# Keeping the last two expert blocks' rows on chip and adding them with one-hot products in the final norm

## The chip, the cores and the metric

The kernel runs on one core of a Trainium2 chip. A core has a matrix engine (TensorE, PE in the profile), a vector engine (VectorE, DVE), an activation engine (ScalarE, ACT), GpSimd (POOL), and SyncE (SP), whose queue starts most transfers. The metric is the device time of one launch in microseconds, as a median of several runs.

## The reference

One transformer block of 1024 latent tokens and 256 context tokens, 1024 wide: a mixer (gated delta rule and a gated recurrence), then a mixture of 32 experts of which each token uses two, and after each of the two a residual sum with a layer norm. Only the last part is touched by the change:

```python
def post_norm(r, g, b):
    return (layer_norm(r) * g + b).astype(r.dtype)
...
    x = post_norm(DEEP_ALPHA * x + gt1_l * u_l, ln_g[l, 0], ln_b[l, 0])
    f_l = hierarchical_moe(modulate(x, sh2_l, sc2_l).reshape(B * L, D), *moe_args).reshape(B, L, D)
    x = post_norm(DEEP_ALPHA * x + gt2_l * f_l, ln_g[l, 1], ln_b[l, 1])
```

The expert sum `f_l` of a token has two terms, one for each expert that it uses, each scaled by its router weight.

## The kernel before

The mixer and the routing take the first 870 us or so and stay as they are. Then come 22 blocks of up to 128 token slots, in the order of the table `ORDER`. A block holds the tokens of one to four experts ("pieces"). For each block the loop of `make`, `up`, `turn` and `down` gathers token rows from DRAM (`gather`, POOL), transposes them (`pf`, `xT`), multiplies by the up weights (`pu`), applies the gate (`hid`), transposes (`hT`) and multiplies by the down weights (`py`). VectorE scales the product by router weight and gate into a tile `y`, in two halves of 512 columns (line 1536).

`acc` is a DRAM tensor of 1024 rows that starts as the scaled residual. `down` adds the rows of `y` to it with one indirect transfer from POOL's queue for each piece (line 1539), each of which reads, adds and writes the rows that the table names (`rows_to`, or `tbri` for a block of one piece). They follow each other: each waits until the one before has landed. The next to last block has two pieces, the last has one.

Behind the blocks stands a loop over overflow blocks (line 1601), whose count of rounds is read on the chip; with these inputs no round is run, but all engines meet there and wait for all transfers and all engines. Behind it, SP loads `acc` as eight tiles of 128 tokens (line 1640, tiles named `u` as they lie in the places of the expert weights), and the final layer norm runs on each tile: sums and squares (`bn_stats` on VectorE, lines 1657 and 1658, or two passes on ScalarE, lines 1650 and 1651), a first pass `(x - mean) * g` (line 1660), the inverse root (`rsqrt_pool`, lines 149 to 157 on GpSimd, for two tiles at once; the last pair on VectorE, lines 129 to 139), and a second pass `x * rs + b` (line 1671 on VectorE, or lines 1668 and 1669 on ScalarE and GpSimd for three tiles). SP stores each half tile (line 1674). The norm's gain and bias rows are loaded ahead of the overflow loop (lines 1632 and 1633).

A scheduler sets the order on each engine from a timing model, so the order of the rows below is the program's, not the code's.

Of the kernel before, what the change touches and what calls it, by code (L numbers as in the profile page):

```python
# [9 lines left out]
F32 = mybir.dt.float32  # L10
# [8 lines left out]
P = 128  # L19
D = 1024  # L20
# [59 lines left out]
YB = 3  # L80
DEPTH = 2
PA = {'ORD': 'x0 z1 x1 g0 z2 z0 x2 x3 g1 g2 g3 z3', 'ZB': 'qvsa', 'ADV1': 1, 'ADV2': 2, 'PER': 1, 'A0': 0, 'SQB': 1, 'GELU': 0, 'GSTG': 1, 'PM': (4, 4), 'HIV': (3, 8, 10, 14, 17, 20, 23), 'LOV': (2, 4, 21), 'C1V': (0, 1, 3, 4, 5, 14, 15, 19, 23), 'PSS': 0, 'TOK': (('kt', 4), ('v', 4)), 'EMV': 0, 'RGV': 0, 'CVB': 3, 'WRB': 3, 'HO': 'kvq', 'SQP': 0, 'YMA': 0}

UNITS = 18

# [2 lines left out]
def hybrid_block(ctx, tc, x, c, ctx_in, c_ctx, w_ada, b_ada, w_in, conv_qkv_w, dn_a_log, dn_dt_bias, dn_onorm_w,  # L88
# [1346 lines left out]
    scs.close()  # L1435
    pss.close()

    psm = ctx.enter_context(tc.tile_pool(name="psm", bufs=1, space=PSUM, reuse_waits="tile"))
    me = ctx.enter_context(tc.tile_pool(name="me", bufs=1, side="right", reuse_waits="tile"))
    more[0] = psm  # L1440
    ptab = psm.tile([P, 512], F32, name="ptab", tag="ptab")
# [16 lines left out]
    route_last()  # L1458
    ri, wslot = rows_of(ptab, NBLK, "tb")
    sb_moe["routed"] = wo  # L1460
    rows_to = T_([P, 4, NBLK - ONE], "rows_to", I32)
    V.tensor_tensor(rows_to, ptab[:, None, ONE:NBLK].to_broadcast([P, 4, NBLK - ONE]), onl, op=ALU.add)

# [8 lines left out]
    class Block:  # L1472
# [50 lines left out]
            self.hT = sb.tile([P, 2, P], F32, name="hT", tag="hT", bufs=2)  # L1523
            nc.scalar.copy(self.hT[:, :, 0:u], pt[:, 0:256].rearrange("p (f t) -> p f t", t=P)[:, :, 0:u])  # L1524

        def down(self, ws):
            u = self.used
            turn = self.in_turn()
            y = sb.tile([P, D], F32, name="y", tag="y", bufs=YB)
            for q in range(2):  # L1530
                qs = slice(q * 512, (q + 1) * 512)
                py = psm.tile([P, 512], F32, name="py", tag="py", bufs=3)
                for f in range(2):
                    for r, o, n in parts(self.pieces):
                        turn(nc.tensor.matmul(py[o:o + n, :], self.hT[:, f, o:o + n], ws[r][:, f, qs], start=f == 0, stop=f == 1))  # L1535
                nc.vector.scalar_tensor_tensor(y[0:u, qs], py[0:u, :], self.weights[0:u], gt2[0:u, qs], op0=ALU.mult, op1=ALU.mult)  # L1536

            for (r, o, n), to in zip(self.pieces, self.to):
                nc.gpsimd.indirect_dma_start(out=acc, out_offset=bass.IndirectOffsetOnAxis(ap=to[0:o + n], axis=0), in_=y[0:o + n], in_offset=None,  # L1539
                                             bounds_check=NL - 1, oob_is_err=False, compute_op=ALU.add)  # L1540

    blocks = []

    def make(i):
        if i < NBLK:
# [9 lines left out]
    for i in range(NBLK + 1):  # L1555
        if i < NBLK:
            blocks[i].up(W)
            ahead(i, i - 2)
        if i > 0:
            blocks[i - 1].down(Wd)  # L1560
            ahead(min(i, NBLK - 1), i - 1)
        if i + 1 < NBLK:
            blocks[i + 1].transpose()
            make(i + 3)
        if i < NBLK:
            blocks[i].turn()
# [68 lines left out]
    for i in range(4):  # L1635
        x2 = place(4 + i, [P, 2, D])
        for q in range(2):
            t = 2 * i + q
            xs.append(x2[:, q, :])
            nc.sync.dma_start(xs[t], acc[t * P:(t + 1) * P, :])  # L1640
    mv = cst.tile([P, 8, 2], F32, name="mv3")
    rs = cst.tile([P, 8], F32, name="rs3")
    for t0 in range(0, 8, 2):
        ts, two = (t0, t0 + 1), slice(t0, t0 + 2)
        for t in ts:
            x_, mean, var = xs[t], mv[:, t, 0:1], mv[:, t, 1:2]
            if t in (3, 5, 6, 7):
                sq = sb.tile([P, D], F32, name="sq2", tag="y", bufs=YB)
                nm = small([P, 1], "nm3")
                nc.scalar.activation(sq, x_, AF.Identity, scale=-1.0 / D, accum_out=nm)  # L1650
                nc.scalar.activation(sq, x_, AF.Square, bias=nm, accum_out=var)
                nc.vector.tensor_scalar_mul(var, var, 1.0 / D)
                nc.vector.tensor_scalar_mul(mean, nm, -1.0)
            else:
                st_ = small([P, 2, 6], "st2")
                for q in range(2):
                    nc.vector.bn_stats(st_[:, q, :], x_[:, q * 512:(q + 1) * 512])  # L1657
                nc.vector.bn_aggr(mv[:, t, :], st_)
        for t in ts:
            nc.vector.scalar_tensor_tensor(xs[t], xs[t], mv[:, t, 0:1], lg1, op0=ALU.subtract, op1=ALU.mult)  # L1660
        if t0 < 6:
            rsqrt_pool(rs[:, two], mv[:, two, 1], 1.0, LN_EPS)
        else:
            rsqrt(rs[:, two], mv[:, two, 1], 2, LN_EPS)
        for t in ts:
            x_ = xs[t]
            if t in (1, 2, 3):
                nc.scalar.activation(x_, x_, AF.Identity, scale=rs[:, t:t + 1])
                nc.gpsimd.tensor_tensor(x_, x_, lb1, op=ALU.add)
            else:  # L1670
                nc.vector.scalar_tensor_tensor(x_, x_, rs[:, t:t + 1], lb1, op0=ALU.mult, op1=ALU.add)  # L1671
            for b in range(2):
                c0 = 64 * (t if (t + b) % 2 == 0 else 15 - t)
                nc.sync.dma_start(out[0, c0:c0 + 64, :], x_[64 * b:64 * b + 64, :])


_INS = ['x', 'c', 'ctx', 'c_ctx', 'w_ada', 'b_ada', 'w_in', 'conv_qkv_w', 'dn_a_log', 'dn_dt_bias', 'dn_onorm_w',
# [35 lines left out]
```

## Time and profile before

| what | value |
|---|---|
| median of 3 runs | 1283.7 us (1281.74 to 1283.74) |
| the profiled execution's own time | 1272.99 us |
| its span in the trace | 1271.3 us |
| TensorE busy | 1092.1 us (86%) |
| VectorE busy | 683.3 us (54%) |
| ScalarE busy | 418.0 us (33%) |
| GpSimd busy | 419.4 us (33%) |

All times of the trace are microseconds from the start of the span. The shares of busy time say little here, since the change touches only the last 70 us or so: what matters is which wait ends last there. In the rows, `x` and a number is the count of merged instructions, and a bracket at the end of a row is the time that the engine stood idle before it and what ended that.

### The profile page before, as it was taken

The page shows a single profiled execution, that of the slowest core. Times are in us where ns is not written, and L with a number is a line of the kernel's source. Part 1 is how long each engine was busy: PE and PEld are TensorE (multiplying, and loading weights), DVE is VectorE, ACT ScalarE, POOL GpSimd, SP SyncE. Part 2 cuts the span into 40 slices and gives each one's busy share as a digit, 9 for nine tenths or more (in the row PEclk, how much of TensorE's full clock was granted, in tenths as well). Part 3 has the DMA queues.
Part 4 walks back from the last instruction along what each step waited for, and adds up shares of the span by engine and source line. Part 5 has one row for each costly group of instructions (what it writes and reads, how often), then busy time and mean ns, then how long its engine had stood idle before and what let it go on. Part 6 is the DMA issues. An engine that isn't in the chain of part 4 may idle for free. (4 is left out here: it accounts for less than half of the span.)

```text
span 1271.3 us, 18178 instructions
## 1 busy us (share of the span) xinstructions
PE 1092.1 (86%) x6674; PEld 693.2 (55%) x6674; DVE 683.3 (54%) x1605; ACT 418.0 (33%) x745; POOL 419.4 (33%) x489
## 2 busy tenths in 40 slices
PE   4899998998999899987999999984999978969810
PEld 1357775776776677764667777664343323323200
DVE  3737479478694975875446766736222212214127
ACT  0534424233322618961222445351221111112003
POOL 1511414232243233453630176552122222222115
PEclk8699999999899999987999999875899989979865
DMA  9413453654446231009886255695899999997855
GB/s 340 161 44 98 141 140 100 183 152 127 134 120 178 66 104 38 17 20 315 263 270 196 96 184 184 247 365 189 295 334 352 334 317 341 317 336 220 271 149 174
DMA packets 147010, 251.40 MB, mean 198 GB/s; under 512 B 36844, under 2 KB 98472, under 8 KB 134632
## 3 DMA queue, kind: packets, MB, share of 16 engines
q1 hardware_dynamic: 132688, 215.94, 51.7%
q0 software_dynamic: 7456, 16.80, 5.8%
q10 hardware_dynamic: 6776, 17.49, 3.6%
q8 instruction: 53, 0.87, 0.3%
q14 instruction: 37, 0.30, 0.1%
HBM read 205.34 MB, written 54.67 MB: 205 GB/s over the span
## 5 line engine op out<-in xcount | busy, mean ns | idle before, releaser
L1513 PE MATMUL pu<-u,xT 128*32 128x512 f32 (+2 forms) x768 | 180.7, 630 | 22.5 <-DVE xT L1495 16.1
L403 PE MATMUL pj<-hhi,whi 128*128 128x512 f32 (+1 forms) x480 | 188.9, 394 | 4.4 <-ACT s L439 2.8
L404 PE MATMUL pj<-hlo,whi 128*128 128x512 f32 (+1 forms) x480 | 186.0, 387 | 0.0
L405 PE MATMUL pj<-hhi,wlo 128*128 128x512 f32 (+1 forms) x480 | 184.4, 385 | 0.0
L1513 PEld LDWEIGHTS pu<-u,xT 128*32 128x32 f32 (+2 forms) x768 | 57.5, 139 | 116.0 <-issue 85.4
L403 PEld LDWEIGHTS pj<-hhi,whi 128*128 128x128 f32 x480 | 92.6, 193 | 49.6 <-issue 18.7
L405 PEld LDWEIGHTS pj<-hhi,wlo 128*128 128x128 f32 x480 | 92.8, 194 | 21.0 <-issue 5.7
L404 PEld LDWEIGHTS pj<-hlo,whi 128*128 128x128 f32 x480 | 92.9, 194 | 19.2 <-issue 5.3
L399 POOL TENSOR_TENSOR wlo<-wraw,whi 128x1024 fp32r<-128x1024 f32 x21 | 52.4, 2496 | 151.7 <-ACT whi L398 115.0
L1539 POOL DMA_INDIRECT acc<-y,rows_to x28 | 41.2, 1472 | 147.4 <-DMA acc<-y,rows_to 81.6
L1536 DVE SCALAR_TENSOR_TENSOR y<-py,tbw,gt 128x512 f32<-128x512 f32 x44 | 32.4, 749 | 105.6 <-DMA acc<-y,rows_to 48.3
L1535 PE MATMUL py<-u,hT 128*32 128x512 f32 (+2 forms) x384 | 82.9, 598 | 4.4 <-ACT hT L1524 2.4
L619 DVE TENSOR_TENSOR s<-s,s 80x31 f32<-80x31 f32 (+15 forms) x124 | 64.4, 520 | 18.6 <-DMA s<-ad 16.1
L434 DVE SCALAR_TENSOR_TENSOR cv<-pj,par,cv 128x504 f32<-128x504 f32 (+3 forms) x96 | 63.9, 668 | 10.7 <-ACT cv L422 9.6
L1516 DVE TENSOR_TENSOR hid<-hid,pu 128x256 f32<-128x256 f32 x22 | 9.1, 419 | 110.8 <-ACT hid L1515 110.8
L1493 ACT ACTIVATE xT<-pf,mod 128x128 f32<-128x128 f32 x88 | 34.7, 455 | 97.3 <-PE pf L1489 92.4
L621 DVE TENSOR_TENSOR s<-s,s 80x31 f32<-80x31 f32 (+15 forms) x124 | 59.3, 478 | 2.3
L403 PE MATMUL pf<-whi,yh 128*128 128x512 f32 x128 | 56.7, 443 | 1.5 <-ACT whi L938 1.1
L405 PE MATMUL pf<-whi,yl 128*128 128x512 f32 x128 | 54.4, 425 | 0.0
L404 PE MATMUL pf<-wlo,yh 128*128 128x512 f32 x128 | 54.3, 425 | 0.0
L1535 PEld LDWEIGHTS py<-u,hT 128*32 128x32 f32 (+2 forms) x384 | 26.5, 132 | 49.6 <-issue 43.0
L1515 ACT ACTIVATE hid<-pu 128x256 f32<-128x256 f32 x22 | 8.3, 384 | 134.5 <-PE pu L1513 134.5
(488 smaller groups left out, 2079.0 us busy)
## 6 DMA issues: line engine op xcount, KB each, us to landing
u<-in_w_up_dram SPq DMA_DIRECT2D x64, 1024.0 KB, 7.7
u<-in_w_down_dram SPq DMA_DIRECT2D x32, 1024.0 KB, 8.4
st<-sp SPq DMA_DIRECT2D x52, 384.0 KB, 5.2
wraw<-in_w_ada_dram SPq DMA_DIRECT2D x32, 512.0 KB, 3.7
wraw<-in_w_in_dram SPq DMA_DIRECT2D x24, 512.0 KB, 5.6
wada<-in_w_ada_dram SPq DMA_DIRECT2D x4, 2048.0 KB, 8.4
sp<-t SPq DMA_DIRECT2D x12, 512.0 KB, 4.5
wor<-in_w_out_dram SPq DMA_DIRECT2D x8, 512.0 KB, 5.9
```

Of the source, the lines that this page charges most:

```text
L399: (nc.vector if i in PA["LOV"] else nc.gpsimd).tensor_tensor(lo, raw, hi.bitcast(F32), op=ALU.subtract)
L403: nc.tensor.matmul(o, lh, rh, start=start, stop=False)
L404: nc.tensor.matmul(o, lh, rl, start=False, stop=False)
L405: nc.tensor.matmul(o, ll, rh, start=False, stop=stop)
L434: nc.vector.scalar_tensor_tensor(yo, xi, w(j), yo, op0=ALU.mult, op1=ALU.add)
L619: nc.vector.tensor_tensor(t_, sa[:, j + 1:32, j:j + 1].to_broadcast([80, n, j + 1]), T[:, j:j + 1, 0:j + 1].to_broadcast([80, n, j + 1]), ...
L621: nc.vector.tensor_tensor(T[:, j + 1:32, 0:j + 1], T[:, j + 1:32, 0:j + 1], t_, op=ALU.subtract)
L1493: nc.scalar.activation(self.xT[:, i, 0:u], pt[:, k * P:k * P + u], AF.Identity, bias=mod2[:, 0, i:i + 1], scale=mod2[:, 1, i:i + 1])
L1513: turn(nc.tensor.matmul(pu[o:o + n, :], self.xT[:, k, o:o + n], ws[r][k // 4][:, k % 4, :], start=k == 0, stop=k == KT - 1))
L1535: turn(nc.tensor.matmul(py[o:o + n, :], self.hT[:, f, o:o + n], ws[r][:, f, qs], start=f == 0, stop=f == 1))
L1536: nc.vector.scalar_tensor_tensor(y[0:u, qs], py[0:u, :], self.weights[0:u], gt2[0:u, qs], op0=ALU.mult, op1=ALU.mult)
L1539: nc.gpsimd.indirect_dma_start(out=acc, out_offset=bass.IndirectOffsetOnAxis(ap=to[0:o + n], axis=0), in_=y[0:o + n], in_offset=None, boun ...
```

## The change

The rows of the last two blocks (`LATE = 2`) are no longer added to `acc` in DRAM. `down` keeps each block's `y` in SBUF as a pair of tiles of a reduced 32-bit type: `keep[0]`, a rounded copy by ScalarE, and `keep[1]`, the rest, by VectorE. A table `oh` of one-hot matrices is made on VectorE: for block i and token tile t, row s of a 128 by 128 matrix has a one in the column of the token that slot s belongs to, and is zero if that token is in another tile. The loaded sums come eight tiles at a time as before; for each, `total` forms in PSUM, for each half of 512 columns, the sum of four products of a one-hot matrix with a kept half (two blocks, two parts), and of the identity with the loaded tile in full 32-bit. The final norm then reads PSUM: two tiles use `bn_stats`, six use the two ScalarE passes, and all eight use VectorE for both last passes and GpSimd for the inverse root, one tile at a time. GpSimd's additions of the bias are gone.

```diff
+LATE = 2
...
+    lrow = T_([P, LATE, 8], "lrow")
+    for i in range(LATE):
+        b = ORDER[NBLK - LATE + i]
+        for t in range(8):
+            V.tensor_scalar(lrow[:, i, t:t + 1], ptab[:, b:b + 1], NONE - float(P * t), None, op0=ALU.add)
...
+            if keep is not None:
+                nc.scalar.copy(keep[0], y)
+                nc.vector.tensor_tensor(keep[1], y, keep[0].bitcast(F32), op=ALU.subtract)
+                return
...
+    oh = pool_of(11).tile([P, LATE, 8, P], F32R, name="u11", tag="u11")
+    for i in range(LATE):
+        for t in range(8):
+            nc.vector.tensor_scalar(oh[:, i, t, :], io128, lrow[:, i, t:t + 1], None, op0=ALU.is_equal)
+    pse.close()
+    psn = ctx.enter_context(tc.tile_pool(name="psn", bufs=1, space=PSUM, reuse_waits="tile"))
...
-            if t in (3, 5, 6, 7):
...
-            if t in (1, 2, 3):
-                nc.scalar.activation(x_, x_, AF.Identity, scale=rs[:, t:t + 1])
-                nc.gpsimd.tensor_tensor(x_, x_, lb1, op=ALU.add)
...
+    def total(t):
+
+        pt = psn.tile([P, 2, 512], F32, name="pn", tag="pn", bufs=3)
+        for q in range(2):
+            qs = slice(q * 512, (q + 1) * 512)
+            for i in range(LATE):
+                for h in range(2):
+                    nc.tensor.matmul(pt[:, q, :], oh[:, i, t, :], keeps[i][:, h, qs], start=i == h == 0, stop=False)
+            nc.tensor.matmul(pt[:, q, :], ident, xs[t][:, qs], start=False, stop=True)
+        return pt
+
+    for t in range(8):
+        pt = total(t)
+        full = pt.rearrange("p q f -> p (q f)")
+        mean, var = mv[:, t, 0:1], mv[:, t, 1:2]
+        if t in (0, 4):
...
+            rsqrt_pool(rs[:, t:t + 1], var, 1.0, LN_EPS)
         else:
...
+            nc.scalar.activation(sq, full, AF.Identity, scale=-1.0 / D, accum_out=nm)
+            nc.scalar.activation(sq, full, AF.Square, bias=nm, accum_out=var)
+            nc.gpsimd.tensor_scalar(mean, nm, -1.0, None, op0=ALU.mult)
+            rsqrt_pool(rs[:, t:t + 1], var, 1.0 / D, LN_EPS)
+        x_ = xs[t]
+        nc.vector.scalar_tensor_tensor(x_, full, mean, lg1, op0=ALU.subtract, op1=ALU.mult)
+        nc.vector.scalar_tensor_tensor(x_, x_, rs[:, t:t + 1], lb1, op0=ALU.mult, op1=ALU.add)
```

In the lists of order, line numbers of the changed kernel are larger (by 2 to 26), and a kernel's weights, kept rows, one-hot table and loaded tiles all bear the name `u`.

POOL, the adding transfers of the last blocks and what follows up to the overflow loop, before and after:

```order
L1539 DMA acc<-y,tbri 1024x1024 x2
L1539 DMA acc<-y,rows_to 1024x1024 x4
L1539 DMA acc<-y,tbri 1024x1024
L1598 TENSOR_LOAD osm
L1601 COMPARE_AND_BRANCH
```

```order
L1552 DMA acc<-y,tbri 1024x1024 x2
L1552 DMA acc<-y,rows_to 1024x1024 x2
L1614 TENSOR_LOAD osm
L1617 COMPARE_AND_BRANCH
L1617 ISA
```

Three of the adding transfers are gone: the two of the next to last block and the one of the last.

TensorE, the next to last and the last block, the end of them before and their middle after (`pu` is an up product, `py` a down product, `pf` transposes; 32-row products belong to the next to last block, 128-row ones to the last):

```order
L1535 MATMUL py<-u_9313,hT 32x512
L1513 MATMUL pu<-u_9407,xT 128x512 x4
L1535 MATMUL py<-u_9367,hT 32x512 x3
L1522 MATMUL pf<-ident,hid 128x128 x2
L1535 MATMUL py<-u_9448,hT 128x512 x4
```

```order
L1521 MATMUL pu<-u_9422,xT 128x512 x4
L1530 MATMUL pf<-ident,hid 128x128 x2
L1521 MATMUL pu<-u_9424,xT 128x512 x4
L1544 MATMUL py<-u_9330,hT 32x512
L1544 MATMUL py<-u_9384,hT 32x512 x3
```

The last block's second four up products stood in front of the last three of the next to last block's down products; now they stand in front of all sixteen, so that the last block's gate can be worked out beside these. Behind the sixteen follow the transposes and the last block's four down products, as before.

GpSimd behind the overflow loop, after only (lines 151 to 159 are one inverse root, 1693 is the mean of a tile; the number of `nm` tells the tile: 9943 is tile 1, 9971 is tile 2):

```order
L1693 TENSOR_SCALAR mv_9902<-nm_9943 128x1
L151 TENSOR_SCALAR rp_u<-mv_9902 128x1
L155 TENSOR_TENSOR rs_9903<-rp_u,half 128x1
L156 TENSOR_TENSOR rp_w<-rs_9903 128x1
L157 TENSOR_TENSOR rp_w<-rp_w,rp_u 128x1
L158 TENSOR_SCALAR rp_w<-rp_w 128x1
L1693 TENSOR_SCALAR mv_9902<-nm_9971 128x1
L159 TENSOR_TENSOR rs_9903<-rs_9903,rp_w 128x1
```

The last step of tile 1's inverse root stands behind the mean of tile 2. From tile 3 on each tile's mean and six steps stand in a row.

## Rows read from the trace of the kernel before

**Rows 1.** Chain of waits, 1213 us to its end: start, length, what

```profile
1213.57 9.10 DMA acc<-y,rows_to
...
1223.41 6.00 DMA acc<-y,tbri
1229.41 0.02 SPq L1601
...
1230.24 3.86 DMA u<-acc
...
1234.13 1.30 DVE st L1657 x2
...
1264.65 1.20 DVEq L1708
```

**Rows 2.** Timeline, last two blocks: start, length, engine, line, operation, tiles, shape

```profile
1194.76 3.46 PE L1513 MATMUL pu<-u,xT 128*128 128x512 f32 x4 [2.27 <-DMA u<-in_w_up_dram]
...
1202.30 0.75 DVE L1536 SCALAR_TENSOR_TENSOR y<-py,tbw,gt 128x512 f32<-128x512 f32 x1 [8.90 <-PE py L1535]
1202.37 1.55 POOL L1539 DMA_INDIRECT acc<-y,rows_to  x1 [2.50 <-DMA acc<-y,rows_to]
...
1209.27 0.41 DVE L1516 TENSOR_TENSOR hid<-hid,pu 128x256 f32<-128x256 f32 x1
...
1209.74 0.44 PE L1522 MATMUL pf<-ident,hid 128*128 128x128 f32 x2 [1.19 <-DVE hid L1516]
1209.87 1.33 POOL L1539 DMA_INDIRECT acc<-y,rows_to  x1 [5.95 <-DVE hid L1516]
...
1210.69 3.70 PE L1535 MATMUL py<-u,hT 128*128 128x512 f32 x8 [0.52 <-ACT hT L1524]
...
1214.43 0.75 DVE L1536 SCALAR_TENSOR_TENSOR y<-py,tbw,gt 128x512 f32<-128x512 f32 x1 [0.97 <-PE py L1535]
```

**Rows 3.** Timeline, final norm, one row of each kind of step

```profile
1238.92 1.06 ACT L1650 ACTIVATE sq<-u 128x1024 f32<-128x1024 f32 x1 [28.29 <-DMA u<-acc]
...
1240.11 1.15 ACT L1651 ACTIVATE sq<-u,nm 128x1024 f32<-128x1024 f32 x1
...
1246.23 1.27 DVE L1660 SCALAR_TENSOR_TENSOR u<-u,mv,u 128x1024 f32<-128x1024 f32 x1
1246.40 1.16 POOL L149 TENSOR_SCALAR rp_u<-mv 128x2 f32<-128x2 f32 x1 [1.24 <-DVE mv L1652]
...
1263.37 2.48 DVE L1671 SCALAR_TENSOR_TENSOR u<-u,rs,u 128x1024 f32<-128x1024 f32 x2
```

**Rows 4.** Timeline of TensorE, in the mixer's projections: products of the reduced 32-bit type

```profile
302.00 0.39 PE L404 MATMUL pj<-hlo,whi 128*128 128x512 f32 x1
302.22 0.39 PE L405 MATMUL pj<-hhi,wlo 128*128 128x512 f32 x1
```

**Rows 5.** Timeline, GpSimd's inverse root of one tile, in the mixer's norms

```profile
779.29 0.69 DVE L977 SCALAR_TENSOR_TENSOR x<-x,pf 128x512 f32<-128x512 f32 x1 [0.92 <-PE pf L405]
779.40 0.19 POOL L155 TENSOR_TENSOR rp_wx<-rp_wx,rp_ux 128x1 f32<-128x1 f32 x1
779.67 0.19 POOL L156 TENSOR_SCALAR rp_wx<-rp_wx 128x1 f32<-128x1 f32 x1
...
822.49 0.55 POOL L153 TENSOR_TENSOR rs2x<-rp_ux,half 128x1 f32<-128x1 f32 x1
...
823.95 0.19 POOL L157 TENSOR_TENSOR rs2x<-rs2x,rp_wx 128x1 f32<-128x1 f32 x1
```

**Rows 6.** Windows: stretch, length, engines' busy time (count), granted clock, DMA share, GB/s

```profile
1195.00:1200.00 5.00, 5.00 (x10) 2.02 (x9) 0.00 (x0) 0.37 (x1) 1.33 (x1) 0.66 0.96 365
...
1215.00:1220.00 5.00, 0.00 (x0) 0.00 (x0) 0.18 (x1) 0.00 (x0) 0.12 (x1) 0.90 0.89 199
1220.00:1225.00 5.00, 0.00 (x0) 0.00 (x0) 0.00 (x0) 0.00 (x0) 1.55 (x1) 0.50 0.21 71
```

**Rows 7.** Timeline, TensorE's first work of the expert stage

```profile
892.30 1.97 PE L1489 MATMUL pf<-ident,xg 128*128 128x128 f32 x8 [5.19 <-DMA xg<-h2d,tbri]
```

More of the change, by code (lines that the diff above doesn't have):

```diff
@@ L1436, in hybrid_block @@
     pss.close()
-    psm = ctx.enter_context(tc.tile_pool(name="psm", bufs=1, space=PSUM, reuse_waits="tile"))
+    pse = ExitStack()
+    psm = pse.enter_context(tc.tile_pool(name="psm", bufs=1, space=PSUM, reuse_waits="tile"))
     me = ctx.enter_context(tc.tile_pool(name="me", bufs=1, side="right", reuse_waits="tile"))
@@ L1524, in turn, with down @@
             nc.scalar.copy(self.hT[:, :, 0:u], pt[:, 0:256].rearrange("p (f t) -> p f t", t=P)[:, :, 0:u])
-        def down(self, ws):
+        def down(self, ws, keep=None):
             u = self.used
@@ L1540, in down @@
                                              bounds_check=NL - 1, oob_is_err=False, compute_op=ALU.add)
-    blocks = []
+    blocks, keeps = [], []
     def make(i):
@@ L1559, in hybrid_block @@
         if i > 0:
-            blocks[i - 1].down(Wd)
+            if i - 1 >= NBLK - LATE:
+                p_ = 8 + i - 1 - (NBLK - LATE)
+                keeps.append(pool_of(p_).tile([P, 2, D], F32R, name=f"u{p_}", tag=f"u{p_}"))
+            blocks[i - 1].down(Wd, [keeps[-1][:, q, :] for q in range(2)] if keeps else None)
             ahead(min(i, NBLK - 1), i - 1)
@@ L1640, in hybrid_block @@
             nc.sync.dma_start(xs[t], acc[t * P:(t + 1) * P, :])
+    oh = pool_of(11).tile([P, LATE, 8, P], F32R, name="u11", tag="u11")
[4 more added lines that the diff above has]
+    psn = ctx.enter_context(tc.tile_pool(name="psn", bufs=1, space=PSUM, reuse_waits="tile"))
     mv = cst.tile([P, 8, 2], F32, name="mv3")
     rs = cst.tile([P, 8], F32, name="rs3")
[L1643 to L1646, printed above, removed]
-            if t in (3, 5, 6, 7):
[L1648 to L1662, printed above, removed]
-        else:
-            rsqrt(rs[:, two], mv[:, two, 1], 2, LN_EPS)
-        for t in ts:
-            x_ = xs[t]
-            if t in (1, 2, 3):
-                nc.scalar.activation(x_, x_, AF.Identity, scale=rs[:, t:t + 1])
-                nc.gpsimd.tensor_tensor(x_, x_, lb1, op=ALU.add)
[L1670 to L1674, printed above, removed]
@@ new lines, in hybrid_block @@
+    sums = []
+    def total(t):
[12 more added lines that the diff above has]
+        if t in (0, 4):
+            st_ = small([P, 2, 6], "st2")
+            for q in range(2):
+                nc.vector.bn_stats(st_[:, q, :], pt[:, q, :])
+            nc.vector.bn_aggr(mv[:, t, :], st_)
+            rsqrt_pool(rs[:, t:t + 1], var, 1.0, LN_EPS)
+        else:
+            sq = sb.tile([P, D], F32, name="sq2", tag="y", bufs=YB)
+            nm = small([P, 1], "nm3")
+            nc.scalar.activation(sq, full, AF.Identity, scale=-1.0 / D, accum_out=nm)
[5 more added lines that the diff above has]
+        nc.vector.scalar_tensor_tensor(x_, x_, rs[:, t:t + 1], lb1, op0=ALU.mult, op1=ALU.add)
+        for b in range(2):
+            c0 = 64 * (t if (t + b) % 2 == 0 else 15 - t)
+            nc.sync.dma_start(out[0, c0:c0 + 64, :], x_[64 * b:64 * b + 64, :])
```

## The prediction

> **What bounds the kernel now.** I read the chain of waits first, then the timelines of the last 80 us, then windows for the clock. The chain [rows 1] shows that the end is not set by any busy engine until 1234 us, but by adding transfers that follow each other: the second piece of the next to last block starts at 1213.57 and is followed for 9.10 us, the last block's starts at 1223.41 and takes 6.00, then SP steps out of the overflow loop and starts the loads of the sums at 1230.24. The first lands 3.86 later, VectorE starts at 1234.13, and its last pass ends at 1264.65 + 1.20 = 1265.85. TensorE's last product had ended at 1210.69 + 3.70 = 1214.39 [rows 2]: it then does nothing, and its granted clock sinks to 0.50 [rows 6]. So the time from 1214.39 to 1230.24, 15.85 us, is waiting for additions in DRAM, and from 1230.24 to 1265.85, 35.6 us, is load and norm. I call the start of the loads T. Behind the last pass the stores take 1271.3 - 1265.85 = 5.45 us, and nothing in the change alters that. The sum is made on the profiled execution (1272.99 us); its difference is carried to the median, which stands 10.7 us higher.
>
> **The change part by part.**
>
> *T moves.* Three adding transfers go, so the loop's waits end with whatever comes next. The adding transfers that stay end with the one issued at 1202.37; when POOL issued the next one at 1209.87, the wait before it was ended by VectorE and not by a transfer [rows 2], so it had landed by then. VectorE and ScalarE: from the end of the next to last block's products (1209.74 - 1.19 = 1208.55) a half of y (0.75), the rounded copy (not in the trace; nearest, a ScalarE pass of the same size, 1.06 [rows 3]), the subtraction (nearest, a VectorE pass of the same size, 1.27) give 1211.6, and the first half of the last block's y 1212.4. TensorE is the last: before, 2.14 us lie between 1208.55 and the last product's start at 1210.69, because the gate's product (0.41 at 1209.27) waits its turn. In the new order the gate is done beside the longer product, and only the transposes (0.44) and the wait for their copy (0.52) remain: 0.96, a gain of 1.2, so TensorE ends at 1213.2. SP's steps out of the loop took 1230.24 - 1229.41 = 0.83 [rows 1]. T = 1214.1; bounds 1213.4 (the steps already made) and 1215.3 (no gain from the order). Moved by 16.1 us, 14.9 to 16.8.
>
> *The loads.* SP now issues two tiles, then the gain and bias rows, which were loaded ahead of the loop, then six tiles. ScalarE's first pass, on the fourth tile, waited for its load until 1238.92 [rows 3], so a tile lands every (1238.92 - 1230.24 - 3.86) / 3 = 1.6 us. The two row loads together are 1 MB, which took some 5 us at 199 GB/s [rows 6], or 3.2 at the tiles' rate: I take 4.2. So tile 0 lands at T + 3.9, tile 1 at 5.5, tile 2 at 11.3, tile 7 at 19.3.
>
> *TensorE.* Products of the reduced type start 0.22 to 0.23 us apart [rows 4]; a full 32-bit one is two passes of 3.70 / 8 = 0.46 [rows 2]. A tile has eight and two: 8 x 0.23 + 2 x 0.92 = 3.7 us, 29 us in all, none of which was there before. Ten of the first products need no load. Behind the loop the second half of y, copy and subtraction (0.75 + 1.06 + 1.27 = 3.1) come first, which ends about when tile 0 lands. Then tile 0 ends at T + 3.9 + 2.8 = 6.7, tile 1 at 9.9, tile 2, whose load comes at 11.3, at 14.1, and then one every 3.7: tile 7 at 32.6.
>
> *Norm of a tile.* ScalarE's two passes take 2.4 (1238.92 to 1241.26 [rows 3]). GpSimd's small steps start 0.27 us apart (779.40, 779.67), and the power takes 0.55: a root is 0.28 to its second step, then from 822.49 to 823.95 + 0.19 another 1.65, in all 1.93, and 0.28 for the mean [rows 5]. VectorE's passes 1.27 and 1.24 [rows 3]. These meet in a ring: a GpSimd step that starts during a pass with both tensors in SBUF lasts until that pass ends (1246.40 + 1.16 against 1246.23 + 1.27 [rows 3]), while one during a pass that reads PSUM took its usual 0.19 (779.40 [rows 5]). Now the first pass reads PSUM and the second does not. So from one tile's second pass to the next: 1.24 (GpSimd held), mean 0.28, root 1.93, some 0.1 for handing over: 3.6 us, as long as TensorE's 3.7. Tile 1's root is held by the order: its last step stands behind the mean of tile 2, so its second pass starts at 14.1 + 1.06 + 0.28 + 0.28 = T + 15.8. Six rings to tile 7: 15.8 + 21.6 = 37.4, and 0.6 more where tile 4's statistics (1.3 on VectorE) stand ahead of tile 3's second pass; end at 38.0 + 1.24 = T + 39.3. By TensorE alone it would be 32.6 + 2.4 + 2.2 + 1.24 = 38.4. Before: T + 35.6. The norm stage gets longer by 3.7 us, though two passes and additions on ScalarE and GpSimd are gone.
>
> *Covered.* The sixteen one-hot rows (at most 0.41 each [rows 2], 6.6 us) are made while VectorE sits idle for 8.90 before 1202.30; without cover they would delay the last gate by up to 6.6. The sixteen small operations on the routing table stand in front of TensorE's wait of 5.19 us for gathered rows [rows 7], for which VectorE is not needed; uncovered, they too cost at most 6.6.
>
> *The clock.* TensorE worked at the lower level for a stretch after it had waited 2.27 us: four passes took 3.46 us against 1.85 at the upper one, mean granted clock 0.66 [rows 2, 6]. Here it waits about 1 us at the loop, then does ten short products in 4 us, and waits again for tile 2. One or two such stretches, 1.6 us each, are to be expected; the first falls into the wait for tile 2 and costs nothing, a second would cost up to 1.6.
>
> The Trainium skill (TensorE: Matmul & The Clock Gate, section "A second HAM failure mode: psum-queue depth-cycling") says that a kernel that cycles through PSUM banks may rest so often between groups of products that the clock swings between its levels. That is the shape of the new norm, three PSUM buffers in turn; the trace before has no such stage, and the forecast lets TensorE stay at the upper level because it is short by only 0.1 us per tile of being the bound. What it would cost is the rival below.
>
> Sum: -16.1 + 3.7 = -12.4. 1272.99 - 12.4 = 1260.6 for the profiled execution, 1283.7 - 12.4 = **1271.3 us** for the median. With the bounds: -16.8 + 2.8 = -14.0 (1269.7) and -14.9 + 3.7 + 1.6 = -9.6 (1274.1); with the uncertainty of the medians themselves (2 us between the runs before), 1268 to 1276.
>
> **The rivals.**
>
> *GpSimd is held by both passes.* For it: all passes of the final norm before held it. Against it: the row with a PSUM input [rows 5]. A ring would be 1.27 longer, seven of them 8.9: -3.5, 1280.2 us.
> The Trainium skill (SBUF, section "SBUF: two separate sides") says that the shared port pair is taken by a VectorE operation with two SBUF inputs; by it, a pass with one input in PSUM leaves GpSimd free, as the row shows.
>
> *The norm is no longer than before.* Loads of the rows at the tiles' rate, the ring shortened by work that I put in series: T + 36, so -15.7, 1268.0 us. For it: GpSimd and ScalarE have less to do, and TensorE can run three tiles ahead.
>
> *Slower: TensorE at the lower level through the norm.* For it: it enters the norm after a rest, and between tiles it waits for PSUM; at rest its clock is at 0.50 [rows 6]. Against it: its work is nearly back to back from tile 2 on. A tile would take 7.4: tile 0 ends at 9.5, tile 1 at 16.0, tile 2 at 21.6, tile 7 at 58.6, the end at T + 64.4: -16.1 + 28.8 = +12.7, 1296.4 us. It decides once half of the tiles run so (12.4 of 25 us).
>
> *It doesn't do what it says.* The adding transfers of both blocks are out of GpSimd's list, so this could only mean that the loop's waits end late for another reason. To bring the time within 0.2%, T would have to be 9.8 us later, so the last remaining adding transfer, issued at 1202.37, would have to land at 1223 instead of before 1209.87; its like took 9.10 in the chain [rows 1].
>
> **How the numbers follow.** Forecast 0.66, norm as long as before 0.12, GpSimd held by both 0.12, slower 0.06, no gain 0.04. A measurement of this kernel can tell about 0.2%, 2.6 us, from no change. Faster: 0.66 + 0.12 + 0.10 of the held case = 0.88; within 0.2%: 0.02 of it and 0.04 = 0.06; slower 0.06. The range for 8 in 10 takes in the forecast's own, the shorter norm to 1267 and the nearer half of the held case to 1279; outside are its far end, no gain and slower.
>
> **What would show it.** Right: the loads start about 16 us earlier, at 1213.4 to 1215.3 after a like course before; the last rows on the chain ahead of them are TensorE's down product instead of adding transfers; a tile's second passes are 3.6 to 3.9 us apart; the last ends 38 to 41 us behind the start of the loads; the granted clock in that stretch is 0.9 or more. Wrong: GpSimd steps of 1.2 us during first passes (held by both), passes of 0.86 instead of 0.46 in the norm (lower level), or a loop that is left late. A shift of more than 3 us before 1190 would be an effect that I don't foresee.

## The result and the profile after

The changed kernel took 1266.9 us (median of 4 runs, 1262.3 to 1272.2) against 1283.7 (4 runs, 1281.7 to 1291.7) measured beside it: ratio 0.986, 95% interval 0.982 to 0.990. It is faster, as forecast; 1266.9 lies just under the low end of the range, 1267. Two later comparisons of the same two kernels gave 0.990 (0.985 to 0.995) and 0.993 (0.989 to 0.996). Weighted by their intervals the three make 0.990, some 13 us (10 to 16). The profiled execution took 1262.33 us, its span is 1260.6.

The timeline around the overflow loop answers to [rows 2] and the end of [rows 1]:

```profile
1204.84 1.33 POOL L1552 DMA_INDIRECT acc<-y,rows_to  x1 [9.13 <-DMA acc<-y,tbri]
...
1209.85 1.55 POOL L1552 DMA_INDIRECT acc<-y,rows_to  x1 [3.69 <-DMA acc<-y,rows_to]
...
1213.80 3.70 PE L1544 MATMUL py<-u,hT 128*128 128x512 f32 x8 [0.52 <-ACT hT L1532]
...
1217.83 0.81 SPq L1656 DMA_DIRECT2D u<-acc  x2
1218.68 0.75 DVE L1545 SCALAR_TENSOR_TENSOR y<-py,tbw,gt 128x512 f32<-128x512 f32 x1 [1.95 <-issue]
1218.69 2.01 SPq L1648 DMA_DIRECT2D u<-in_ln_g_dram  x1
```

The last down product ends at 1213.80 + 3.70 = 1217.50, the loads of the sums start 0.33 later; before, 15.85 us lay between. The two adding transfers left at the end are over by then. The chain of waits (start, length, what) from there on:

```profile
1218.68 0.76 DVE y L1545
...
1219.64 3.82 PE pn L1674 x10
1223.46 1.21 PE pn L1675 x2
1224.67 0.93 PE pn L1674 x4
1225.60 0.86 PE pn L1675 x2
...
1242.08 0.87 PE pn L1675 x2
1243.03 1.12 ACT sq L1691 x2
...
1252.61 0.20 POOL rp_u L151
...
1254.58 1.28 DVE u L1697
```

No DMA is in it. Where the chain of before ran from an adding transfer to the load of the sums and then over VectorE, this one runs over TensorE: half a tile is four one-hot products in 0.93 us and two passes of the identity product in 0.86, so 3.58 a tile. From 1243.03 on the chain shows ScalarE, GpSimd and VectorE, though TensorE works on until 1250.08: ScalarE's passes on the last two tiles, at 1246.61 and 1250.18, start both 0.10 behind the end of the tile's sum and 0.02 to 0.04 behind a step of GpSimd, so this chain alone cannot tell which they waited for; e6 and e11 below do. In windows (stretch, length, busy time of PE, PEld, DVE, ACT, POOL, granted clock, DMA share, GB/s) TensorE is busy without a gap from 1226 on, at its upper level (1.00). Soon after its stand at the loop it worked for some 3 us at the lower level (0.50 in the second row), the clock that it has at rest in [rows 6]:

```profile
1218.00:1226.00 8.00, 6.36 (x19) 4.43 (x19) 1.98 (x2) 1.05 (x1) 0.00 (x0) 0.79 0.87 279
...
1221.00:1223.00 2.00, 2.00 (x6) 1.51 (x6) 0.77 (x1) 0.00 (x0) 0.00 (x0) 0.50 1.07 379
...
1226.00:1250.00 24.00, 24.00 (x80) 14.57 (x78) 18.90 (x19) 11.60 (x20) 12.67 (x44) 1.00 0.73 239
```

The norm's steps in the timeline, which answer to [rows 3, 5]:

```profile
1228.07 1.28 DVE L1696 SCALAR_TENSOR_TENSOR u<-pn,mv,u 128x1024 f32<-128x1024 f32 x1
...
1228.40 0.58 POOL L155 TENSOR_TENSOR rs<-rp_u,half 128x1 f32<-128x1 f32 x1
...
1229.06 0.19 POOL L156 TENSOR_TENSOR rp_w<-rs 128x1 f32<-128x1 f32 x1
...
1230.10 1.28 DVE L1697 SCALAR_TENSOR_TENSOR u<-u,rs,u 128x1024 f32<-128x1024 f32 x1 [0.75 <-POOL rs L159]
...
1230.81 0.68 POOL L1693 TENSOR_SCALAR mv<-nm 128x1 f32<-128x1 f32 x1 [0.74 <-ACT sq L1691]
```

GpSimd's steps keep their length during the first pass, which reads PSUM (L1696), and the mean that starts during the second pass ends with it (1230.81 + 0.68 against 1230.10 + 1.28). That is what the forecast took from [rows 5].

The span became 1271.3 - 1260.6 = 10.7 us shorter. The loads start 1230.24 - 1217.83 = 12.4 earlier, although the last product ended 3.1 later than before (1217.50 against 1214.39); from the loads' start to the end of the last pass it is 1255.86 - 1217.83 = 38.0 instead of 35.6; the stores behind it take 4.7 instead of 5.45. -12.4 + 2.4 - 0.7 = -10.7.

### The profile page after: what moved, and what is told of

It reads as the page before. It is cut to its first block, busy times and chain, and to the rows that moved or that the text cites. A ratio compares the mean times of both kernels' runs of the same rounds, so it can differ in the third digit from the quotient of the medians.

```text
span 1260.6 us, 18437 instructions
## 1 busy us (share of the span) xinstructions
PE 1124.0 (89%) x6770; PEld 715.9 (57%) x6770; DVE 683.4 (54%) x1617; ACT 421.0 (33%) x752; POOL 412.5 (33%) x519
## 5 line engine op out<-in xcount | busy, mean ns | idle before, releaser
L1521 PE MATMUL pu<-u,xT 128*32 128x512 f32 (+2 forms) x768 | 177.9, 632 | 31.4 <-DVE xT L1503 17.4
L1552 POOL DMA_INDIRECT acc<-y,rows_to x26 | 38.4, 1475 | 139.6 <-DMA acc<-y,rows_to 76.9
L621 DVE TENSOR_TENSOR s<-s,s 80x31 f32<-80x31 f32 (+15 forms) x124 | 65.3, 527 | 14.5 <-DMA s<-ad 11.9
```

Source lines behind the costliest of these rows:

```text
L621: nc.vector.tensor_tensor(t_, sa[:, j + 1:32, j:j + 1].to_broadcast([80, n, j + 1]), T[:, j:j + 1, 0:j + 1].to_broadcast([80, n, j + 1]), ...
L1521: turn(nc.tensor.matmul(pu[o:o + n, :], self.xT[:, k, o:o + n], ws[r][k // 4][:, k % 4, :], start=k == 0, stop=k == KT - 1))
```

## The experiments

To compare executions whose earlier parts differ, I take four points of each profile: S, the issue of the first adding transfer of the third block from the end; E, the end of the last down product; T, the start of the loads of the sums; L, the end of the last pass. The last column is from E to the end of the span. All times are us. Every row is one profiled execution; e6, e9, e10 and e11 were run once each, so their times say nothing.

| run | E - S | T - S | T - E | L - T | E to end |
|---|---|---|---|---|---|
| before, profiled | 15.9 | 31.7 | 15.85 | 35.6 | 56.9 |
| before, e5 | 10.7 | 31.3 | 20.6 | 37.5 | 63.5 |
| before, e9 | 16.2 | 28.2 | 12.0 | 35.5 | 53.0 |
| changed, profiled | 12.7 | 13.0 | 0.33 | 38.0 | 43.1 |
| changed, e1 | 11.4 | 11.7 | 0.32 | 38.0 | 43.1 |
| changed, e10 | 8.1 | 11.3 | 3.2 | 36.5 | 44.5 |
| changed, e12 | 11.8 | 12.2 | 0.33 | 38.0 | 43.1 |
| e2, transfers left out, old norm | 12.6 | 13.0 | 0.33 | 37.0 | 42.9 |
| e3, new norm alone | 10.4 | 31.2 | 20.7 | 33.6 | 59.1 |
| e4, last block alone kept | 11.9 | 24.0 | 12.0 | 33.5 | 50.3 |
| e6, four one-hot products a tile | 15.0 | 15.6 | 0.65 | 35.7 | 41.1 |
| e7, products first, no mean step | 5.7 | 11.6 | 5.9 | 37.0 | 47.6 |
| e8, two sums on VectorE | 15.0 | 15.3 | 0.32 | 40.5 | 45.6 |
| e11, twelve one-hot products a tile | 11.5 | 11.9 | 0.33 | 43.7 | 48.8 |

**e1: the changed kernel again.**

> The changed kernel once more, unaltered. Theory (what the two profiled executions differ by is the gain; the medians of few runs scatter by up to 10 us around it): the ratio comes out near 1 - 12/1283 = 0.990, and the runs of either kernel again spread over about 10 us. Rival (the first comparison, 1266.9 against 1283.7, is the gain, so something beyond the moved loads and the longer norm was saved): 0.987 or less. In the profile both expect the loads of the sums about 0.3 us behind the last down product, and the last pass 38.0 us behind them; where the last product ends may differ by several us from execution to execution, and the weights' stream should show where (waits for in_w_up_dram between 1060 and 1200).

The ratio was 0.990 (0.985 to 0.995): the middle is the theory's, the interval takes in the rival's 0.987 too. This kernel's runs went from 1267 to 1279, those of before from 1275 to 1299 (29 runs). T and L came as expected. In the profile the weights' waits differ: the next to last block's up products started at 1195.35 after a wait of 7.97 us for `in_w_up_dram`, in the first profile at 1189.81 after 3.21.

**e2: the start of the loads alone.**

```diff
             for (r, o, n), to in zip(self.pieces, self.to):
+                if drop:
+                    break
...
-            blocks[i - 1].down(Wd)
+            blocks[i - 1].down(Wd, i - 1 >= NBLK - 2)
```

> The kernel before with the three adding transfers of the last two blocks left out and nothing put in their place, so their rows are missing from the output; the norm is the old one. It prices the moved start T alone. Theory (the path to T was the chain of adding transfers, 1214.39 to 1230.24): T comes within 1 us behind the last down product, some 15 to 16 us earlier than in before, the norm keeps its 35.6 us (up to 3 more if the row loads of gain and bias now go behind T), and the time is 1268 to 1272, ratio 0.988 to 0.991. Rival 1 (the time between is the loop's own exit or a transfer of another kind): T stays more than 5 us behind the last product and the gain is under 10 us. Rival 2 (the new norm saved time too, so that more than half of the first comparison's 16.8 us isn't T): ratio 0.993 or more.

The gain and bias loads moved behind the loop, as in the changed kernel, though the edit doesn't touch them. From the timeline, the last product and SP's queue:

```profile
1215.08 3.70 PE L1535 MATMUL py<-u,hT 128*128 128x512 f32 x8 [0.52 <-ACT hT L1524]
...
1219.11 1.04 SPq L1642 DMA_DIRECT2D u<-acc  x2
1220.19 0.63 SPq L1634 DMA_DIRECT2D u<-in_ln_g_dram  x1
```

T is 0.33 behind E and E to end is 42.9, the changed kernel's 43.1 within 0.2. The time, 0.993 (0.990 to 0.997), is at rival 2's edge and can't tell it from the theory. The profile can: with the transfers gone, the old norm ends as early as the new one, which also adds the rows. The timed gain, 8.5 us (4 to 13), is less than the 14.9 by which E to end differs from the mean of before, 57.8; that mean stands on three executions between 53.0 and 63.5, so the two don't contradict each other, but they don't confirm each other either.

**e3: the new norm alone** (`LATE = 0`, without `lrow` and `oh`, identity products only).

> All adding transfers stay as in before; only the norm is the new one, its sums in PSUM made by the identity product alone (the tile's one-hot products have nothing to add and are gone). It prices the new norm without its sixteen one-hot products a block. TensorE then has 1.7 to 1.9 us a tile. Theory A (TensorE's 3.57 us a tile sets the changed norm's pitch): the pitch falls to VectorE's two passes and what holds GpSimd, 2.6 to 3.2 us, the last pass ends 30 to 34 us behind T, and the time is 2 to 5 us below before, ratio 0.996 to 0.9985. Theory B (the ring of second pass, mean and root, 3.6 us, as the forecast had it, sets it as well): pitch 3.5 to 3.7, last pass T + 37 to 39, ratio 1.001 to 1.003.

L - T is 33.6, the last second passes are 3.12 apart: theory A. The time, 0.999 (0.996 to 1.003), does not settle it, and in this execution T came 20.7 behind E. The new norm without one-hot products is 2 to 4 us shorter than the old one (35.5 to 37.5); with eight a tile it gives that back.

**e4: only the last block kept** (`LATE = 1`).

> Only the last block stays on chip (one adding transfer less instead of three); TensorE has four one-hot and two identity products a tile, 2.7 us. Theory (each adding transfer at the end is a step of a chain: 6.0 us for the last block's, 9.1 for the second piece before it): T comes 6 to 7 us earlier than in before, behind the second piece of the next to last block, the norm takes T + 33 to 36, and the time is 6 to 10 us below before, ratio 0.992 to 0.995. Rival (the chain's last step alone held everything, and the other two hide behind the last block): T within 1 us of the last down product, ratio like the changed kernel's, 0.987 to 0.990.

0.992 (0.988 to 0.996). E to end is 50.3, between 53 to 63 before and 43 to 44.5 for two blocks; L - T is 33.5, no longer than with no one-hot product at all. T - S is 24.0 against 28.2 to 31.7 before: as the theory has it, each transfer is a step of the chain. T is 12.0 behind E, so the rival, by which only the last transfer held the loop, does not hold. The last transfer and the loads:

```profile
1234.54 1.55 POOL L1552 DMA_INDIRECT acc<-y,rows_to  x1 [4.49 <-DMA acc<-y,rows_to]
...
1241.53 3.89 SPq L1656 DMA_DIRECT2D u<-acc  x8
```

**e5: before again.**

> The kernel before once more, unaltered, for a profile of another execution (the one that the prediction was summed on, 1272.99, is faster than all 29 timed since). I count from the end of the last block's down product to the end of the program: 56.9 us in the profiled execution of before, 43.1 in both of the changed kernel, so 13.8 saved. Theory (the chain of adding transfers behind the last product is longer in a usual execution, because more of it is still queued when that product ends, as with the new norm alone, where the loads started 20.7 behind it instead of 15.85): the last product ends later than 1214.4, the loads start 17 to 21 us behind it and the count is 58 to 62. Rival (all executions of before differ only ahead of the last product): loads 15.5 to 16.2 behind it, count 56.5 to 57.3, and a timed gain beyond 13.8 is scatter.

The chain of waits of this execution:

```profile
1215.49 1.55 DMA acc<-y,rows_to
...
1222.49 1.33 POOL acc L1539
...
1228.85 6.17 DMA acc<-y,rows_to
...
1235.76 6.49 DMA acc<-y,tbri
...
1243.08 0.33 SPq L1640
```

TensorE ended at 1222.52, and the first of the three transfers of the last two blocks was issued only then, at 1222.49; in [rows 2] it was out 4.5 us before TensorE ended (1209.87 against 1214.39). In both it came 7.0 to 7.5 us behind the transfer before it (1215.49, 1202.37), and in e9 7.1, whatever TensorE did. T - E is 20.6, as the theory had it. The count, 63.5, is above its 58 to 62 since the norm was longer too, by 1.9 us. What made it so is a load: the statistics of the second tile start 7.1 us behind T here and 5.3 in the first profile, and from there to the end of the last pass both take 30.3. VectorE's rows, the first profile and this one:

```profile
1235.58 1.23 DVE L1657 BATCH_NORM_STATS2 st<-u 128x6 f32<-128x512 f32 x2
```

```profile
1250.22 1.29 DVE L1657 BATCH_NORM_STATS2 st<-u 128x6 f32<-128x512 f32 x2 [1.59 <-DMA u<-acc]
```

The eight runs of this comparison are the same kernel as the 25 beside them, and their ratio is 1.003 (0.998 to 1.007): the medians lie 3.2 us apart with no edit at all. Further on the timeline has two rows that all three executions of before share:

```profile
1257.28 2.57 POOL L1669 TENSOR_TENSOR u<-u,u 128x1024 f32<-128x1024 f32 x1 [1.26 <-ACT u L1668]
1257.57 3.37 DVE L1660 SCALAR_TENSOR_TENSOR u<-u,mv,u 128x1024 f32<-128x1024 f32 x1
```

VectorE's pass took 3.37 instead of 1.27 while GpSimd added the bias (3.37 and 3.36 in the other two executions). The change takes these additions out.

**e6: four one-hot products a tile.**

```diff
-                for h in range(2):
+                for h in range(1):
                     nc.tensor.matmul(pt[:, q, :], oh[:, i, t, :], keeps[i][:, h, qs], start=i == h == 0, stop=False)
```

> The changed kernel with only the rounded high part of the kept rows added (their low parts are left out): four one-hot products a tile instead of eight, so TensorE has 2.7 us a tile instead of 3.57. Everything else stays. Theory (in the changed kernel TensorE sets the norm's pitch; without it GpSimd's ring does, 3.2 us as with one block kept): a second pass every 3.1 to 3.3 us, the last pass ends 34 to 35.5 us behind the start of the loads instead of 38.0. Rival (the ring of 3.6 us, as the forecast had it, sets it too, since with one block kept the start was another): 3.5 to 3.7 and 37.5 to 38.

The last second passes:

```profile
1262.34 1.28 DVE L1697 SCALAR_TENSOR_TENSOR u<-u,rs,u 128x1024 f32<-128x1024 f32 x1 [0.64 <-POOL rs L159]
...
1265.46 1.28 DVE L1697 SCALAR_TENSOR_TENSOR u<-u,rs,u 128x1024 f32<-128x1024 f32 x1 [0.64 <-POOL rs L159]
```

They are 3.12 apart, as expected; L - T is 35.7, a little above the theory's 34 to 35.5, far from the rival's 37.5.

**e11: twelve one-hot products a tile.**

```diff
-                for h in range(2):
+                for h in (0, 1, 0):
```

> The changed kernel with the high part's one-hot product made twice (the kept rows' high part is added a second time, so the sums are other ones): twelve one-hot products a tile instead of eight, 0.9 us more of TensorE. Theory (TensorE sets the changed norm's pitch): 4.4 to 4.5 us a tile and a last pass 38.0 + 7 = 44.5 to 46 us behind T. Rival (GpSimd's ring of 3.6 us sets it as much): the pitch rises only by what TensorE exceeds it, the last pass ends 41.5 to 43.5 behind T.

```profile
1260.29 1.28 DVE L1699 SCALAR_TENSOR_TENSOR u<-u,rs,u 128x1024 f32<-128x1024 f32 x1 [0.67 <-POOL rs L159]
...
1264.78 1.28 DVE L1699 SCALAR_TENSOR_TENSOR u<-u,rs,u 128x1024 f32<-128x1024 f32 x1 [0.68 <-POOL rs L159]
```

The pitch, the distance between the second passes of two tiles, is 4.49, the theory's. L - T, 43.7, lies between the two expectations, 0.2 above the rival's and 0.8 below the theory's; what made it shorter is not shown. With zero or four one-hot products the last pitch is 3.1, with eight 3.57 (in all four profiles of the changed kernel), with twelve 4.49. So TensorE sets it from eight on, and below that something else does, at 3.1.

**e7: an attempt at a shorter norm.** All one-hot products of three tiles first, no mean step, statistics of the last tile on VectorE:

```diff
+    for i in range(LATE):
+        for t in range(FIRST):
+            ahead_ = onehot(t, i)
...
-        if t in (0, 4):
+        if t in (0, 7):
...
-            nc.gpsimd.tensor_scalar(mean, nm, -1.0, None, op0=ALU.mult)
...
+            nc.vector.scalar_tensor_tensor(x_, full, nm, lg1, op0=ALU.add, op1=ALU.mult)
```

> The changed kernel with three edits in the norm: all 24 one-hot products of the first three tiles stand ahead of the first identity product; the first pass adds the negative mean as ScalarE made it, without GpSimd's step in between; the last tile's statistics are taken on VectorE, the fifth's on ScalarE. Theory (TensorE is the bound, and idles between the loop and the first tile's load): up to 14 products of 0.23 us more fit into that wait, but they can't start before the last block's low part is there; 1 to 2 us saved, another 1 at the last tile; the last pass ends 35 to 36.5 us behind the start of the loads instead of 38.0, the count from the last down product's end is 40 to 41.5 instead of 43.1. Rival (GpSimd's ring is the bound): the mean's step, 0.2 to 1.0 us a tile, goes too, 33 to 34.5. Rival (TensorE at its lower level after the rest eats the wait): 37 to 38.

The time was 0.991 (0.987 to 0.996), no better than the changed kernel's. L - T is 37.0, outside the theory's 35 to 36.5; and e10, where the loads also waited for a transfer, had 36.5 without any of these edits. No gain is shown. The second rival, TensorE at its lower level, comes nearest: the granted clock is 0.51 in the first 4 us behind T, and the 24 products took 1.6 us longer than the same 24 in e8, where it is 1.00. The two rows, e7 and e8:

```profile
1228.25 7.32 PE L1672 MATMUL pn<-u,u 128*128 128x512 f32 x24 [6.37 <-issue]
```

```profile
1233.51 5.74 PE L1673 MATMUL pn<-u,u 128*128 128x512 f32 x24 [2.14 <-DVE y L1545]
```

From the first second pass to the last it was 22.5 us, against 24.4 to 24.5 in the four profiles of the changed kernel, so the edits shortened the later part, and the start took that back. With the one-hot products of three tiles done, TensorE is ahead for a while, and the run shows what the 3.1 is made of:

```profile
1247.13 1.28 DVE L1716 SCALAR_TENSOR_TENSOR u<-u,rs,u 128x1024 f32<-128x1024 f32 x1 [0.61 <-POOL rs L159]
...
1250.22 1.28 DVE L1716 SCALAR_TENSOR_TENSOR u<-u,rs,u 128x1024 f32<-128x1024 f32 x1 [0.61 <-POOL rs L159]
```

```profile
1247.18 1.29 POOL L151 TENSOR_SCALAR rp_u<-mv 128x1 f32<-128x1 f32 x1
1248.55 0.55 POOL L155 TENSOR_TENSOR rs<-rp_u,half 128x1 f32<-128x1 f32 x1
...
1250.00 0.19 POOL L159 TENSOR_TENSOR rs<-rs,rp_w 128x1 f32<-128x1 f32 x1
```

A second pass holds the first step of the next root (1.29 instead of 0.19), five more steps follow, and the next second pass starts: 3.09 us. The mean, which this run leaves out, is hardly on this ring: e6, which has it, is at 3.12.

**e8: two of the sums on VectorE.**

```diff
+        if t in SUMV:
+            nc.vector.tensor_tensor(xs[t], pt.rearrange("p q f -> p (q f)"), xs[t], op=ALU.add)
+            return pt
```

> The kernel of the run before this one, in which the loaded sums of two of the eight tiles are added by VectorE from PSUM (1.28 us each) instead of by TensorE's identity products (1.7 us each). Theory (TensorE is the bound): 2 to 3.4 us less, last pass 32.5 to 34.5 us behind the start of the loads, count 37.5 to 39.5. Rival (VectorE becomes the bound: eight tiles of 2.56, two sums of 1.28, statistics of 3.0, 26 us, and it waits in order): within 1 us of the run before.

0.995 (0.991 to 0.999), L - T 40.5: worse than either expectation. The timeline of VectorE shows why:

```profile
1242.13 1.23 DVE L1680 TENSOR_TENSOR u<-pn,u 128x1024 f32<-128x1024 f32 x1 [6.50 <-DMA u<-acc]
1243.27 1.28 DVE L1706 BATCH_NORM_STATS2 st<-pn 128x6 f32<-128x512 f32 x2
```

The scheduler put the third tile's sum ahead of the first tile's statistics, and VectorE waited for that tile's load until T + 10.4. A second loss comes later, where TensorE stood for a VectorE pass and then took 3.65 us for eight products instead of 2.42, at a granted clock of 0.54:

```profile
1256.04 3.65 PE L1673 MATMUL pn<-u,u 128*128 128x512 f32 x8 [3.37 <-DVE u L1719]
```

What TensorE saved was lost at these two places, so whether VectorE could carry the sums in another order is not answered.

**e9 and e10: another look at each.**

> The kernel before, a third profiled execution. Call S the issue of the third block from the end's first adding transfer, E the end of the last down product, T the start of the loads. So far T - S is 31.7 and 31.3 us in before and 31.2 with the new norm alone, while E - S was 15.9, 10.7 and 10.4. Theory (the five last adding transfers of before are one queue that runs through from S, whenever TensorE ends): T - S is 31 to 32 again, whatever E - S is. Rival (the transfers wait for the last two blocks' rows, so T follows E): T - E is 15.5 to 16.5 or 20 to 21 with T - S elsewhere.

> The changed kernel, a third profiled execution. Theory: T is 0.3 to 0.7 us behind the later of E and the landing of the last transfer that stays, S + 11.2 (T - S was 11.55 where that transfer came last); the last pass ends 38.0 us behind T, as twice before. Rival: the norm's length follows what came before it and differs by more than 0.5 us.

Neither expectation of e9 held: T - S is 28.2, T - E 12.0. In all three executions of before the five transfers are issued one behind the other, 3.6 to 9.8 us apart, but the chain's length varies by 3.5 us: here the last one was issued 6.8 us behind the one before it, in the first profile 9.8, and in e5 the one before took 6.4 instead of 3.7. What makes one of them land later stays open. In e10 the last transfer left landed at 1222.42, behind the end of the last product at 1219.90, and the loads started 0.65 later, as expected; the norm was shorter by 1.5 us, as the rival had it. The chain of waits there:

```profile
1215.50 6.92 DMA acc<-y,rows_to
1222.42 1.07 issue
1223.49 4.05 PE pn L1674 x10
1227.54 0.87 PE pn L1675 x2
```

The first identity product starts 4.5 us behind T there (1227.54), 5.6 in the first profile of the changed kernel: TensorE was at work again 0.4 us behind T instead of 1.8. Before it, it had stood at the loop for 3.6 us.

**e12: the changed kernel's time once more.**

> The changed kernel once more, for its time: two comparisons so far gave 0.986 (0.982 to 0.990) and 0.990 (0.985 to 0.995). Counted in the profiles, from the end of the last down product to the end of the program, before has 53.0, 56.9 and 63.5 us and the changed kernel 43.1, 43.1 and 44.5, a mean difference of 14.2; from the issue of the third block from the end's first adding transfer it is 72.0 against 54.3, 17.8. Theory (the gain is what the end of the program lost, 14 to 18 us): ratio 0.986 to 0.989. Rival (the forecast's sum, 12.4 us, with one execution's chain taken for all): 0.990 to 0.991. Rival (something ahead of the last blocks gains or loses too): outside 0.984 to 0.992. The loads start 0.3 to 0.7 us behind the later of the last down product and the last adding transfer that stays; the last pass ends 36.5 to 38.0 behind them.

The ratio was 0.993 (0.989 to 0.996): the middle lies just outside 0.984 to 0.992, where the second rival has it, but the interval takes in the 0.990 of the forecast's sum and the theory's 0.989, so the run excludes none of the three. The loads and the last pass came as expected. With three comparisons at 0.986, 0.990 and 0.993, the gain is known to some 3 us: 13, with 10 to 16 about it. The count from S, 17.6 us with this execution (72.0 before, 54.4 changed), lies outside; that from E, 14.3 (57.8 and 43.5), lies inside.

## Why the prediction was right and where it was off

The direction and the mechanism were right: three adding transfers set the start of the loads, they are gone, and the norm pays part of it back. The measured 1266.9 lies just outside the range, and two sizes were wrong.

The first is in the last step, which carried the profiled difference to the median: it gave the medians 2 us of uncertainty, from the spread of three runs that happened to lie together, and took 2.6 us to be enough to tell a change from none. The runs showed 5 to 7 us either way for each comparison, and 3.2 us between two medians of the same kernel (e5). The 80 runs of before timed later go from 1274 to 1305, the 18 of the changed kernel from 1265 to 1286, so a median of four moves by several us by itself, and a range that ends 4.3 us below its middle was too short on that side. The later two comparisons, carried to the forecast's 1283.7, would be 1270.6 and 1274, both inside it.

The second is the norm's term: +3.7 us, and nothing for the stores behind it, where the means of the profiles have +1.4 and -0.7. With all terms as measured the sum is -14.4 and the forecast 1269.3, inside the range too, so this term alone did not put the time outside it.

That the forecast of -12.4 agrees with the 13 us of the three comparisons is in part luck: T's term and the norm's were off in opposite ways, and the forecast was read from one execution of before with a T - E of 15.85, where three executions range from 12.0 to 20.6. The profiled execution of before, 1272.99, was at the fast edge of all of them, which was the warning: it stood 10.7 us under its own median.

Step by step:

*T moves.* Forecast -16.1. Means of the profiles: T - E 16.1 before (12.0 to 20.6), 1.04 in the changed kernel (0.32 to 3.2), so -15.1. TensorE's gap in front of the last product shrank as forecast: from the end of the next to last block's products, 1212.91 (1209.27 + 3.64), to 1213.80 are 0.9 us, forecast 0.96. The way out of the loop took 0.33 instead of 0.83. Missed: that the transfers that stay can end behind TensorE. The forecast took them as landed by then; in e10 and e7 they were not, and T stood 3.2 and 5.9 us behind E. The row at 1209.87 in [rows 2] that it read shows only that a transfer had landed 7.5 us behind its issue. In e10 and e7 the last one landed 6.9 and 7.2 us behind its issue; at that pace, as an estimate, the one issued at 1209.85 in the first profile of the changed kernel landed 0.4 to 0.7 us before E (those of e1 and e12 0.5 to 1.2). So the transfers that stay are nearly as late as TensorE, and ending TensorE's work sooner would by this estimate bring about a microsecond at most.

*TensorE.* Forecast 3.7 us a tile and the last product's end at T + 32.6; measured 3.57 and 1249.06 + 1.02 - 1217.83 = 32.3. No tile waited for its load behind the gain and bias rows.

*The ring.* Forecast 3.6 us, measured 3.1 where TensorE doesn't cover it. Here the norm's term went wrong: I added the pass that holds GpSimd (1.24), the mean (0.28) and a whole root (1.93). The step that is held is itself the first of the root, and the mean runs beside it. Since TensorE's pitch was near 3.6 anyway, the error in the end of the last pass is small: T + 38.0 instead of T + 39.3. The rest of the term's error is the norm of before, forecast as the 35.6 of one profile, where three have a mean of 36.2, and e10, whose norm was 1.5 shorter.

*Behind the last pass.* "Nothing in the change alters that" was wrong by 0.7 us: it is 5.4 to 5.6 us in the four profiles with the old norm and 4.7 to 4.8 in the ten with the new one. The likely cause, not tested, is that the last two second passes stood back to back (2.48 in [rows 3]) and four stores met; now they are 3.57 apart.

*Covered work.* The sixteen one-hot rows lay between 1198.87 and 1202.43, while TensorE waited for weights until 1201.99; no wait of the expert stage was ended by them.

*Rivals.* GpSimd held by both passes: no, see the row at 1228.40; the trace agrees here with the Trainium skill (SBUF — State Buffer, "SBUF: two separate sides"). TensorE at the lower level: only at the start. Its first ten products behind the stand at the loop took 3.82 us (0.38 each, where the later ones take 0.23), with the granted clock at 0.50 from 1221 to 1223; from 1226 on it is 1.00. The forecast had one such stretch fall into the wait for tile 2 at no cost; here it lay ahead of the first tile's sum, and what it cost there was not separated. The rule of the Trainium skill (TensorE: Matmul & The Clock Gate, "A second HAM failure mode: psum-queue depth-cycling") did not bear on the norm from 1226 on, which had no pauses between its groups of products. Norm as long as before: nearer than I gave it. The means of L - T are 36.2 before and 37.7 after, +1.4 instead of the forecast's +3.7, and with the stores +0.7. The sum of means is -15.1 + 0.7 = -14.4 where I had -12.4: the term of the norm, +3.7 and +0 for the stores, was mis-sized by three, that of T by one the other way.

Whether 13 or 14.4 is nearer stays open: the runs scatter too much to tell.

## What to carry to other kernels

Before a difference is carried from a profile to a median, look at how far the profiled execution lies from that median: where it is ten us off, the wait that is being removed has another length in other executions, and the range must take in the scatter of both medians. When a chain of transfers is cut short, price what then comes last, the transfers that stay as well as the engine. And count a held step once: what an engine does while it is held is part of the work that follows.

## What the runs showed of the hardware

Executions of one kernel spread over 24 us (22 of the changed one) and 31 us (84 of before). No single place makes it: the expert stage's first up product started between 894.2 and 899.2 us in the seven profiles of the two kernels, and from there to E it took 320 to 332 us. The waits for weights differ, as in e1; what sets them differently was not tried.

The contention of VectorE and GpSimd goes both ways: GpSimd's small steps were held to the end of a VectorE pass with SBUF operands (1.29 instead of 0.19), and a VectorE pass that started 0.29 us into a GpSimd addition took 3.37 instead of 1.27, ending 1.1 us behind it. The Trainium skill (SBUF — State Buffer, "SBUF: two separate sides") calls the shared pair an exclusive lock that the first comer keeps; both rows agree.
